# A two-FFN encoder layer on one core: plain weights ahead of the input sums, split first loads, a written order for the last tile

## The chip, the core and the metric

The kernel runs on one NeuronCore of a Trainium2 chip. The core has five engines that run side by side, each with its own queue of instructions in a fixed order: TensorE (PE) multiplies matrices into PSUM banks, with a separate weight load (PEld) ahead of each product; VectorE (DVE), ScalarE (ACT) and GpSimd (POOL) work elementwise; SyncE (SP) only issues transfers. ScalarE and GpSimd issue transfers as well. Engines wait for each other by semaphores. The metric is the device time of one execution in microseconds; lower is better.

## The reference, cut to what matters

One macaron encoder layer on two sequences of 256 rows that share all weights, so that the kernel works on 512 rows at once: an FFN with half weight, a mixer, a second FFN with half weight, and a final norm. Everything is float32.

```python
def swiglu(h, w_in, w_out):
    a, g = jnp.split(h @ w_in, [D_FF], axis=-1)       # D_FF = 2816
    return (jax.nn.silu(a) * g) @ w_out
...
    x = x + 0.5 * swiglu(rmsnorm(x, g_ffn1), w_ffn1_in, w_ffn1_out)   # x is 512 x 1024
    h = rmsnorm(x, g_mix)
    ...                                                # two scans and a gated merge
    x = x + merged.astype(x.dtype) @ w_out
    x = x + 0.5 * swiglu(rmsnorm(x, g_ffn2), w_ffn2_in, w_ffn2_out)
...
    return rmsnorm(x, g_final)
```

## The kernel before

Activations lie transposed, features on the partitions: eight tiles x0 to x7 of 128 x 512, columns 0 to 255 for one sequence and 256 to 511 for the other. A float32 product is made of three TensorE passes: weights and activations are split into a rounded half (`...h`) and a correction (`...l`), and `mm3` adds h·h, h·l and l·h. The split of a weight tile is either a ScalarE cast and a VectorE subtraction (`split2`), or (`split_dma`) a ScalarE cast, a ScalarE negated cast into the correction tile and a transfer from GpSimd's queue that adds the weights from DRAM to it; only after that transfer has landed may TensorE read the correction.

An FFN (`ffn`, called for the stages f1 and f2) has 22 pairs of output tiles (gate and value). Four parts of it matter here:

- `first_tiles`: the first three pairs (six tiles) over k = 0 to 7, as x arrives; the row scales r come from a sum of squares (`rms_stat`: GpSimd adds the squares, TensorE sums over partitions, VectorE and ScalarE take 1/sqrt, TensorE spreads the result). In f1 this part is at the program's start, where x and the first weights (`raw1`) are loaded, and where ten products on a tile of ones (`warm`) go ahead.
- two *plain* pairs (j = 3 and 4): four products of 24 matmuls each (`plain`), with weights from `w_plain`. Their tiles are p0, p1 (first pair) and p20, p21 (second).
- the other pairs (`pair`, s5 to s21 in the tile names): seven products of half width on sums of blocks of x and of weights, a fast scheme that needs `x_sums` (xc tiles) and `w_sums`. Each product is 12 matmuls. A pair issues five products and leaves the last two (`finish`) to the next pair, so the first pair has five of its own.
- the output tiles (`out_tile`), after each third of the pairs.

Weight tiles come from four rings of two buffers: `raw` and `sum` for what is loaded, `wa` and `wb` for what is split. A new tile of a ring waits until TensorE has read the last product of the tile two before it. A pair of seven products takes one buffer of each. Before, a plain pair's first tile is in wa and its second in wb:

```python
        raws = (stage["raw"].tile([P, 3, T], F32, tag="raw", name=f"raw_{name}"),
                stage["sum"].tile([P, 3, T], F32, tag="sum", name=f"sum_{name}"))
...
                      for p in w_pair("wb" if n else "wa", 2 if n else 5, f"{name}{n}"))
```

The order of the instructions on each engine is set by a scheduler when the program is built; `tc.high_priority`, `tc.issue_after(ins)` (queue behind `ins` on its engine) and `tc.manual_schedule` (keep the written order) direct it.

The last output tile of f2 (`last2`) is cut into the two column halves. Each half has 21 matmuls (`ps_f2l`), a sum of squares (`st_f`), small VectorE steps to 1/sqrt, a diagonal (`dg_f`) and its spread (`sp_f`), and four output tiles y that VectorE scales and that SP and ScalarE send out in turn.

Of the kernel before, what the change touches and what calls it, by code (L numbers as in the profile page):

```python
# [9 lines left out]
F32 = mybir.dt.float32  # L10
# [5 lines left out]
P = 128  # L16
# [20 lines left out]
def encoder_kernel(ctx: ExitStack, tc: tile.TileContext, xT, par, w2, gnorm, mask,  # L37
# [117 lines left out]
    def rms_cols(parts, cs, name, bank=None):  # L155

        ps = scp(f"st_{name}", (P, len(cs))) if bank is None else bank[:, :len(cs)]
        for i, c in enumerate(cs):
            for n, p in enumerate(parts):
                nc.tensor.matmul(ps[:, i:i + 1], lhsT=p[:, c * P:(c + 1) * P], rhs=ones[:, 0:1],  # L160
                                 start=n == 0, stop=n == len(parts) - 1)
        r = small(f"rc_{name}", len(cs))
        rsqrt(r, ps, 1.0 / D, name)
        return r

    def spread(r, name, bank=None):

# [4 lines left out]
        ps = scp(f"sp_{name}", (P, n * P)) if bank is None else bank  # L172
        nc.tensor.matmul(ps, lhsT=ones, rhs=dg.rearrange("p c t -> p (c t)"), start=True, stop=True)
        return ps

# [46 lines left out]
    def split2(hi, lo, src):  # L222
        nc.scalar.copy(hi, src)
        nc.vector.tensor_tensor(out=lo, in0=src, in1=hi.bitcast(F32), op=ALU.subtract)
# [7 lines left out]
    def first_tiles(raws, xs_of, dma_from, name):  # L232
# [3 lines left out]
        for kp in range(4):  # L236
# [3 lines left out]
            for i in range(2):  # L240
# [4 lines left out]
                if kp < dma_from:  # L245
# [14 lines left out]
        return pss, xs  # L260

    def x_sums(gcol, r, name):
# [4 lines left out]
        for k in range(4):  # L267
# [15 lines left out]
            for n, src in enumerate((v, t, w)):  # L283
                hl = [slab(f"xc{p}_{name}{k}{n}", F32R) for p in "hl"]
                split2(*hl, src)
# [6 lines left out]
    def w_sums(w_a, j, name):  # L292
# [8 lines left out]
        nc.gpsimd.dma_start(al[:, 0:2].rearrange("p a b -> p (a b)"), w_a[2 * j], accum_op=ALU.add)  # L301
        nc.vector.tensor_tensor(out=sm[:, 1], in0=sm[:, 0], in1=raw[:, 2], op=ALU.add)
# [25 lines left out]
    def w_plain(w_a, j, name):  # L328

        raws = (stage["raw"].tile([P, 3, T], F32, tag="raw", name=f"raw_{name}"),  # L330
                stage["sum"].tile([P, 3, T], F32, tag="sum", name=f"sum_{name}"))
        res = []
        for n, raw in enumerate(raws):
            raw = raw[:, 0:2].rearrange("p a b -> p (a b)")
            nc.sync.dma_start(raw, w_a[2 * j + n])
            hi, lo = (p.rearrange("p a b -> p (a b)")[:, :2 * T]
                      for p in w_pair("wb" if n else "wa", 2 if n else 5, f"{name}{n}"))
# [13 lines left out]
    def ffn(w_a, w_o, xs_of, raws, dma_from, gcol, sq, name, done, last=None):  # L351
# [3 lines left out]
        late = []  # L355
# [13 lines left out]
        def pair(j, w):  # L369
# [4 lines left out]
            nc.scalar.copy(m[:, L], y[:, :SEQ])  # L374
# [71 lines left out]
        for _ in range(3):  # L446
            next(steps)
# [601 lines left out]
```

## Time and profile before

| | |
|---|---|
| median of 3 runs | 1207.92 us (1207.36 to 1208.99) |
| the profiled execution, its own time | 1207.96 us |
| its span in the trace, first to last instruction | 1206.2 us |
| TensorE busy | 1177.4 us, 98% of the span |
| VectorE, ScalarE, GpSimd busy | 61%, 50%, 10% |
| read from HBM | 135.51 MB, 114 GB/s over the span |

Times in the rows are microseconds from the span's start. The profiled execution is 1.8 us longer than its span, the same amount in a comparison of the two kernels, so sums over the span can be set against its own time. A product's busy time is modelled to its end, past the start of the next; how fast products go is read from their starts. PEclk is the granted clock of TensorE as a share of 2.4 GHz; it has two levels, 1.00 and 0.50 (1.2 GHz).

### The profile page before, as it was taken

The page shows a single profiled execution, that of the slowest core. Times are in us where ns is not written, and L with a number is a line of the kernel's source. Part 1 is how long each engine was busy: PE and PEld are TensorE (multiplying, and loading weights), DVE is VectorE, ACT ScalarE, POOL GpSimd, SP SyncE. Part 2 cuts the span into 40 slices and gives each one's busy share as a digit, 9 for nine tenths or more (in the row PEclk, how much of TensorE's full clock was granted, in tenths as well). Part 3 has the DMA queues.
Part 4 walks back from the last instruction along what each step waited for, and adds up shares of the span by engine and source line. Part 5 has one row for each costly group of instructions (what it writes and reads, how often), then busy time and mean ns, then how long its engine had stood idle before and what let it go on. Part 6 is the DMA issues. An engine that isn't in the chain of part 4 may idle for free.

```text
span 1206.2 us, 16870 instructions
## 1 busy us (share of the span) xinstructions
PE 1177.4 (98%) x6651; PEld 1019.8 (85%) x6651; DVE 736.0 (61%) x1127; ACT 609.0 (50%) x989; POOL 114.9 (10%) x130
## 2 busy tenths in 40 slices
PE   8999999999999998999999999999989999999996
PEld 6798899899987887888888888888879899989985
DVE  6974576567547888657573453463585467566643
ACT  6753365256536655575762332244555256336541
POOL 4100000000021004020000000013100000000011
PEclk9999999999999999999999999999989999999997
DMA  7853555356414214232253223232754356446512
GB/s 236 192 137 112 130 141 139 116 132 164 125 53 127 88 37 131 71 105 70 79 184 114 91 93 114 81 94 44 184 141 130 101 134 156 132 119 154 139 46 70
DMA packets 57952, 141.88 MB, mean 118 GB/s; under 512 B 5320, under 2 KB 19656, under 8 KB 57872
## 3 DMA queue, kind: packets, MB, share of 16 engines
q1 hardware_dynamic: 47904, 110.38, 29.4%
q0 software_dynamic: 8160, 28.06, 13.4%
q10 hardware_dynamic: 1808, 2.36, 0.6%
q8 instruction: 52, 0.85, 0.3%
q14 instruction: 28, 0.23, 0.1%
HBM read 135.51 MB, written 2.11 MB: 114 GB/s over the span
## 4 chain that ended last, share of the span: by engine, by line
PE 89%; DVE 5%; DMA 2%; issue 2%; ACT 1%; SPq 1%; POOL 0%; POOLq 0%; DVEq 0%
PE psy_f L318 16%; PE psq_f L318 8%; PE psz_f L318 4%; PE ps_f1o L203 3%; PE ps_f1o L204 3%; PE ps_f1o L202 3%; PE ps_f2o L203 3%; PE ps_f2o L202 3%; PE ps_f2o L204 3%; PE ps_f2i L258 3%; PE pt_ga L545 2%; PE pt_ga L543 2%; PE pt_ga L544 2%; PE pt_gb L545 2%; PE pt_gb L543 2%; PE pt_gb L544 2%
## 5 line engine op out<-in xcount | busy, mean ns | idle before, releaser
L318 PE MATMUL psy_f<-xch_f,wal_f1s 128*128 128x256 f32 x204 | 57.3, 281 | 0.0
L318 PE MATMUL psy_f<-xcl_f,wah_f1s 128*128 128x256 f32 x204 | 57.2, 281 | 0.0
L318 PE MATMUL psy_f<-xch_f,wah_f2s 128*128 128x256 f32 x204 | 57.2, 281 | 0.0
L318 PE MATMUL psy_f<-xcl_f,wah_f2s 128*128 128x256 f32 x204 | 57.2, 281 | 0.0
L318 PE MATMUL psy_f<-xch_f,wal_f2s 128*128 128x256 f32 x204 | 57.2, 280 | 0.0
L318 PE MATMUL psy_f<-xch_f,wah_f1s 128*128 128x256 f32 x204 | 57.2, 281 | 0.0
L543 PE MATMUL pt_ga<-whi_ga,xh_m 128*128 128x512 f32 x128 | 50.7, 396 | 0.0
L545 PE MATMUL pt_ga<-whi_ga,xl_m 128*128 128x512 f32 x128 | 50.7, 396 | 0.0
L545 PE MATMUL pt_gb<-whi_gb,xl_m 128*128 128x512 f32 x128 | 50.5, 396 | 0.0
L544 PE MATMUL pt_ga<-wlo_ga,xh_m 128*128 128x512 f32 x128 | 50.4, 394 | 0.0
L543 PE MATMUL pt_gb<-whi_gb,xh_m 128*128 128x512 f32 x128 | 50.4, 394 | 0.0
L544 PE MATMUL pt_gb<-wlo_gb,xh_m 128*128 128x512 f32 x128 | 50.4, 394 | 0.0
L94 DVE TENSOR_TENSOR wlo_ga<-raw_ga,whi_ga 128x1024 fp32r<-128x1024 f32 x16 | 19.6, 1224 | 46.0 <-ACT whi_ga L93 46.0
L404 DVE SCALAR_TENSOR_TENSOR x<-ps_f2o,x 128x512 f32<-128x512 f32 x23 | 15.8, 689 | 41.6 <-PE ps_f2o L204 41.6
L93 ACT CAST whi_gb<-raw_gb 128x1024 fp32r<-128x1024 f32 x16 | 16.8, 1048 | 45.7 <-PE pt_ga L545 29.5
L94 DVE TENSOR_TENSOR wlo_gb<-raw_gb,whi_gb 128x1024 fp32r<-128x1024 f32 x16 | 19.6, 1222 | 32.7 <-ACT whi_gb L93 32.6
L318 PEld LDWEIGHTS psy_f<-xch_f,wah_f1s 128*128 128x128 f32 x204 | 38.4, 189 | 0.1
L318 PEld LDWEIGHTS psy_f<-xcl_f,wah_f2s 128*128 128x128 f32 x204 | 38.4, 188 | 0.1
L318 PEld LDWEIGHTS psy_f<-xcl_f,wah_f1s 128*128 128x128 f32 x204 | 38.4, 188 | 0.1
L318 PEld LDWEIGHTS psy_f<-xch_f,wal_f1s 128*128 128x128 f32 x204 | 38.5, 189 | 0.0
L318 PEld LDWEIGHTS psy_f<-xch_f,wah_f2s 128*128 128x128 f32 x204 | 38.3, 188 | 0.1
L318 PEld LDWEIGHTS psy_f<-xch_f,wal_f2s 128*128 128x128 f32 x204 | 38.4, 188 | 0.0
(1155 smaller groups left out, 4039.1 us busy)
## 6 DMA issues: line engine op xcount, KB each, us to landing
raw_f1s<-in_w_f SPq DMA_DIRECT2D x17, 512.0 KB, 3.7
wal_f1s<-in_w_f POOLq DMA_DIRECT2D x17, 512.0 KB, 5.5
raw_f2s<-in_w_f SPq DMA_DIRECT2D x17, 512.0 KB, 3.7
wal_f2s<-in_w_f POOLq DMA_DIRECT2D x17, 512.0 KB, 5.7
raw_ga<-in_w_tm SPq DMA_DIRECT2D x16, 512.0 KB, 3.6
raw_gb<-in_w_tm SPq DMA_DIRECT2D x16, 512.0 KB, 3.6
sum_f1s<-in_w_f SPq DMA_DIRECT2D x17, 256.0 KB, 3.3
raw_f1s<-in_w_f SPq DMA_DIRECT2D x17, 256.0 KB, 4.0
```

Of the source, the lines that this page charges most:

```text
L93: nc.scalar.copy(hi[:, :width], raw[:, :width])
L94: nc.vector.tensor_tensor(out=lo[:, :width], in0=raw[:, :width], in1=hi.bitcast(F32)[:, :width], op=ALU.subtract)
L202: nc.tensor.matmul(ps, lhsT=wh, rhs=xh, start=start, stop=False)
L203: nc.tensor.matmul(ps, lhsT=wh, rhs=xl, start=False, stop=False)
L204: nc.tensor.matmul(ps, lhsT=wl, rhs=xh, start=False, stop=stop)
L258: nc.tensor.matmul(pss[m], lhsT=w[:, f[m]], rhs=xp, start=k == n == 0, stop=k == KD - 1 and n == 2)
L318: nc.tensor.matmul(ps, lhsT=l[:, f], rhs=m, start=start and k == n == 0, stop=stop and k == 3 and n == 2, skip_group_check=True)
L404: nc.vector.scalar_tensor_tensor(out=x[i], in0=ps, scalar=0.5, in1=x[i], op0=ALU.mult, op1=ALU.add)
L543: nc.tensor.matmul(pss[t], lhsT=xh, rhs=hi[:, ws], start=k == 0, stop=False)
L544: nc.tensor.matmul(pss[t], lhsT=xh, rhs=lo[:, ws], start=False, stop=False)
L545: nc.tensor.matmul(pss[t], lhsT=xl, rhs=hi[:, ws], start=False, stop=k == KD - 1)
```

## The change

Four things are changed, three of them in both FFNs.

`w_plain` makes a plain pair's first tile in wb and its second in wa, and `ffn` writes the first plain pair's weights ahead of the input sums and the second's ahead of their last part. The weights of the first seven-product pair (s5) are queued on VectorE behind the last input sum (`issue_after(sums_done)`). Of the second (s6), the loads and the first split (`w_rows`) stay where they were, and the sums are queued on ScalarE behind the first pair's copy m. For k = 0 the weights' split is cut into two halves of three tiles.

At the start x0 comes on SP, the first half of the first weights and the parameters `pt` on ScalarE's queue, an activation on one column loads ScalarE's table early, there are 14 warming products, and the first rounded tile xh_a0 is made on VectorE.

In the last tile the order is written out: both halves' matmuls, the first half's statistics among the second half's matmuls, then the second half's statistics, and only then the outputs of both.

```diff
-    nc.scalar.dma_start(x[0], xT[0:P, :])
-    nc.gpsimd.dma_start(pt, par)
     for k in range(KD):
-        if k:
-            nc.sync.dma_start(x[k], xT[k * P:(k + 1) * P, :])
-        nc.sync.dma_start(raw1[k // 2][:, k % 2], w_f1[0:NF, :, k * P:(k + 1) * P].rearrange("m p f -> p m f"))
+        nc.sync.dma_start(x[k], xT[k * P:(k + 1) * P, :])
+        for n in ((range(0, 3), range(3, NF)) if k == 0 else (range(NF),)):
+            (nc.scalar if k == n[0] == 0 else nc.sync).dma_start(
+                raw1[k // 2][:, k % 2, n[0]:n[-1] + 1],
+                w_f1[n[0]:n[-1] + 1, :, k * P:(k + 1) * P].rearrange("m p f -> p m f"))
+        if k == 0:
+            nc.scalar.dma_start(pt, par)
+
+    act0 = cp.tile([P, 1], F32, name="act0")
+    nc.scalar.activation(act0, ones[:, 0:1], AF.Copy, scale=2.0)
 
     warm = scp("warm", (P, P))
-    for _ in range(10):
+    for _ in range(14):
...
-        nc.scalar.activation(hi, x[k], AF.Copy, scale=col(gcol + k))
+        if name == "a" and k == 0:
+            nc.vector.tensor_scalar(out=hi, in0=x[k], scalar1=col(gcol + k), scalar2=None, op0=ALU.mult)
+        else:
+            nc.scalar.activation(hi, x[k], AF.Copy, scale=col(gcol + k))
...
-                if kp < dma_from:
+                if k == 0:
+                    for h in (slice(0, 3 * P), slice(3 * P, NF * P)):
+                        split2(whi[:, h], wlo[:, h], raw[:, i, h])
+                elif kp < dma_from:
                     split2(whi, wlo, raw[:, i])
...
-        raws = (stage["raw"].tile([P, 3, T], F32, tag="raw", name=f"raw_{name}"),
-                stage["sum"].tile([P, 3, T], F32, tag="sum", name=f"sum_{name}"))
         res = []
-        for n, raw in enumerate(raws):
-            raw = raw[:, 0:2].rearrange("p a b -> p (a b)")
+        for n, (get, pool, w) in enumerate(((w_sum, "wb", 2), (w_raw, "wa", 5))):
+            raw = get(f"{name}{n}")[:, 0:2].rearrange("p a b -> p (a b)")
             nc.sync.dma_start(raw, w_a[2 * j + n])
...
         steps = x_sums(gcol, r, name)
-        for _ in range(3):
+        w_p = w_plain(w_a, NP, f"{name}p")
+        for _ in range(4):
             next(steps)
-        w_p = w_plain(w_a, NP, f"{name}p")
-        next(steps)
         gated(top, pss[2 * top], pss[2 * top + 1])
+        w_p2 = w_plain(w_a, NP + 1, f"{name}p2")
         xc += next(steps)
+        sums_done = x_last[0]
         plain(banks[0], w_p)
-        w_p = w_plain(w_a, NP + 1, f"{name}p2")
         gated(0, pss[0], pss[1])
-        nxt = units[0][0]()
+        with tc.issue_after(sums_done):
+            nxt = units[0][0]()
...
-            cur, nxt = nxt, units[n + 1][0]() if n + 1 < len(units) else None
-            run(cur)
+            cur = nxt
+            if n == 0:
+                j = NP + 3
+                rows = w_rows(w_a, j, f"{name}s{j}")
+                run(cur)
+                with tc.issue_after(copied[0]):
+                    nxt = w_sums(w_a, j, f"{name}s{j}", rows)
+            else:
+                nxt = units[n + 1][0]() if n + 1 < len(units) else None
+                run(cur)
...
+        with tc.manual_schedule(engines={nc.tensor.engine, nc.vector.engine, nc.scalar.engine}):
+            mms(0, range(n))
+            final(0)
+            mms(1, range(n // 2 + 1))
+            st = [rms_sum([sq_of("f"), sql], (0, 1), "f0")]
+            mms(1, range(n // 2 + 1, n))
+            rc = [small(f"rc_f{half}", 2) for half in range(2)]
+            rsqrt(rc[0], st[0], 1.0 / D, "f0")
+            final(1)
+            dg = [diag(rc[0], "f0")]
+            st.append(rms_sum([sq_of("f"), sql], (2, 3), "f1"))
+            rf = [broadcast(dg[0], "f0")]
+            rsqrt(rc[1], st[1], 1.0 / D, "f1")
+            dg.append(diag(rc[1], "f1"))
+            rf.append(broadcast(dg[1], "f1"))
+            for half in range(2):
+                scaled(half, rf[half])
```

`rms_sum`, `diag`, `broadcast` and `w_rows` are parts of `rms_cols`, `spread` and `w_sums`, cut out so that they can be called apart. `mms`, `final` and `scaled` are the three parts of the old loop over the halves.

How the order on the engines moves, at three places. First TensorE in the second FFN, where the second plain product ends and the third begins (ps_f2p1 is the second's bank, ps_f2p2 the third's). Before:

```order
L202 MATMUL ps_f2p1_7648<-xh_b7_7454,wbh_f2p1_7729 128x512
L203 MATMUL ps_f2p1_7648<-xl_b7_7455,wbh_f2p1_7729 128x512
L204 MATMUL ps_f2p1_7648<-xh_b7_7454,wbl_f2p1_7730 128x512
L202 MATMUL ps_f2p2_7875<-xh_b0_7171,wah_f2p20_7840 128x512
L203 MATMUL ps_f2p2_7875<-xl_b0_7172,wah_f2p20_7840 128x512
L204 MATMUL ps_f2p2_7875<-xh_b0_7171,wal_f2p20_7841 128x512
```

and with the change:

```order
L220 MATMUL ps_f2p1_7659<-xh_b7_7463,wah_f2p1_7690 128x512
L221 MATMUL ps_f2p1_7659<-xl_b7_7464,wah_f2p1_7690 128x512
L222 MATMUL ps_f2p1_7659<-xh_b7_7463,wal_f2p1_7691 128x512
L220 MATMUL ps_f2p2_7886<-xh_b0_7180,wbh_f2p20_7778 128x512
L221 MATMUL ps_f2p2_7886<-xl_b0_7181,wbh_f2p20_7778 128x512
L222 MATMUL ps_f2p2_7886<-xh_b0_7180,wbl_f2p20_7779 128x512
```

The order of the four products was wa, wb, wa, wb and is wb, wa, wb, wa, so the second pair's wa tile is read last.

Second, ScalarE in the second FFN around the first and second seven-product pairs (f2s5, f2s6: their weights; f20hh to f24hh: activations of the first five pairs; f2m5, f2u5: copies of the first seven-product pair out of PSUM). Before:

```order
L431 ACTIVATE f2t3_7945<-f2t3_7945 128x512
L299 CAST wah_f2s6_7970<-raw_f2s6_7965 128x1024
L223 CAST f20hh_7931<-f2t0_7851 128x512
L431 ACTIVATE f2t4_7955<-f2t4_7955 128x512
L300 ACTIVATE wal_f2s6_7971<-raw_f2s6_7965 128x1024
L223 CAST f21hh_7936<-f2t1_7925 128x512
L223 CAST wah_f2s6_7970<-sum_f2s6_7966 128x1536
L223 CAST f22hh_7941<-f2t2_7760 128x512
L223 CAST wbh_f2s6_7972<-raw_f2s6_7965 128x1024
L223 CAST f23hh_7951<-f2t3_7945 128x512
L374 COPY f2m5_7986<-psy_f25_7984 128x256
L223 CAST f24hh_7961<-f2t4_7955 128x512
```

and with the change:

```order
L456 ACTIVATE f2t4_7966<-f2t4_7966 128x512
L241 CAST f22hh_7952<-f2t2_7771 128x512
L241 CAST f23hh_7962<-f2t3_7956 128x512
L322 CAST wah_f2s6_7981<-raw_f2s6_7976 128x1024
L323 ACTIVATE wal_f2s6_7982<-raw_f2s6_7976 128x1024
L399 COPY f2m5_7990<-psy_f25_7988 128x256
L241 CAST wah_f2s6_7981<-sum_f2s6_7977 128x1536
L241 CAST f24hh_7972<-f2t4_7966 128x512
L402 ACTIVATE f2t5_7992<-f2t5_7992 128x256
L241 CAST wbh_f2s6_7983<-raw_f2s6_7976 128x1024
L406 COPY f2u5_7991<-psy_f25_7988 128x256
```

The four casts of the second pair's weights moved from before the activations to behind them, with the first pair's copies m and u between and behind them.

Third, VectorE in the last tile (x7: the last tile of x, one half at a time; the number behind f is the half). Before:

```order
L944 SCALAR_TENSOR_TENSOR x7_85<-ps_f2l1_10833,x7_85 128x256
L149 TENSOR_SCALAR v_f0_10807<-st_f0_10801 128x2
L150 RECIPROCAL rc_f0_10806<-s_f0_10808 128x2
L946 TENSOR_TENSOR sql_10776<-x7_85 128x256
L151 TENSOR_TENSOR s_f0_10808<-rc_f0_10806 128x2
L152 SCALAR_TENSOR_TENSOR s_f0_10808<-s_f0_10808,v_f0_10807 128x2
L153 SCALAR_TENSOR_TENSOR rc_f0_10806<-s_f0_10808,rc_f0_10806 128x2
L171 TENSOR_SCALAR dg_f0_10815<-pt_77,rc_f0_10806 128x128 x2
L952 TENSOR_TENSOR y00_10820<-xg00_10562,sp_f0_10818 128x512
```

and with the change:

```order
L158 SCALAR_TENSOR_TENSOR rc_f0_10841<-s_f0_10844,rc_f0_10841 128x2
L982 SCALAR_TENSOR_TENSOR x7_85<-ps_f2l1_10789,x7_85 128x256
L984 TENSOR_TENSOR sql_10787<-x7_85 128x256
L179 TENSOR_SCALAR dg_f0_10853<-pt_77,rc_f0_10841 128x128 x2
L154 TENSOR_SCALAR v_f1_10863<-st_f1_10856 128x2
L155 RECIPROCAL rc_f1_10842<-s_f1_10864 128x2
L156 TENSOR_TENSOR s_f1_10864<-rc_f1_10842 128x2
L157 SCALAR_TENSOR_TENSOR s_f1_10864<-s_f1_10864,v_f1_10863 128x2
L158 SCALAR_TENSOR_TENSOR rc_f1_10842<-s_f1_10864,rc_f1_10842 128x2
L179 TENSOR_SCALAR dg_f1_10871<-pt_77,rc_f1_10842 128x128 x2
L992 TENSOR_TENSOR y00_10876<-xg00_10573,sp_f0_10861 128x512
```

The first half's small steps no longer wait for the second half's x7, and the second half's small steps stand ahead of the first output y00 where they stood behind the fourth.

## Rows read from the trace of the kernel before

**Rows 1.** The page's busy time by engine over the whole span.
```profile
PE 1177.4 (98%) x6651; PEld 1019.8 (85%) x6651; DVE 736.0 (61%) x1127; ACT 609.0 (50%) x989; POOL 114.9 (10%) x130
```

**Rows 2.** TensorE's waits over the span: total us, times, longest us.
```profile
PE ps_f2p L204 <- DMA wal_f2p<-in_w_f: 4.9, 1, 4.9
...
PE sp_f L173 <- DVE dg_f L171: 4.6, 2, 2.6
```

**Rows 3.** Timeline of the second FFN: start us, us, engine, line, operation, [idle before].
```profile
856.64 0.85 POOL L230 DMA_DIRECT2D wbl_f2p<-in_w_f  x1 [3.43 <-ACT xch_f L223]
...
869.99 0.69 DVE L302 TENSOR_TENSOR sum_f2s<-sum_f2s,raw_f2s 128x512 f32<-128x512 f32 x1 [10.90 <-DMA raw_f2s<-in_w_f]
...
875.50 1.05 ACT L229 ACTIVATE wal_f2p<-raw_f2p 128x1024 fp32r<-128x1024 f32 x1
...
876.85 0.85 POOL L230 DMA_DIRECT2D wal_f2p<-in_w_f  x1 [16.31 <-ACT wal_f2p L229]
...
884.51 0.80 PE L204 MATMUL ps_f2p<-xh_b,wal_f2p 128*128 128x512 f32 x1 [4.93 <-DMA wal_f2p<-in_w_f]
...
889.77 0.39 PE L204 MATMUL ps_f2p<-xh_b,wal_f2p 128*128 128x512 f32 x1
```

**Rows 4.** One stretch of the windows view: busy by engine, PEclk, DMA share, GB/s.
```profile
886.00:888.00 2.00, 2.00 (x6) 1.61 (x5) 2.00 (x5) 0.00 (x0) 0.00 (x0) 0.50 0.97 254
```

**Rows 5.** Timeline of the first FFN: the wait among the plain products.
```profile
60.54 0.50 PE L204 MATMUL ps_f1p<-xh_a,wal_f1p 128*128 128x512 f32 x1 [1.76 <-DMA wal_f1p<-in_w_f]
```

**Rows 6.** Timeline of the first FFN's first two pairs of seven products.
```profile
72.73 0.28 PE L318 MATMUL psz_f<-xch_f,wah_f1s 128*128 128x256 f32 x1
...
78.60 1.05 ACT L299 CAST wah_f1s<-raw_f1s 128x1024 fp32r<-128x1024 f32 x1 [0.99 <-PE psy_f L318]
...
79.81 0.28 PE L318 MATMUL psz_f<-xch_f,wah_f1s 128*128 128x256 f32 x1
...
81.17 0.85 POOL L301 DMA_DIRECT2D wal_f1s<-in_w_f  x1 [11.78 <-ACT wal_f1s L300]
```

**Rows 7.** Tile view of wal_f1s: its transfers from issue to landing.
```profile
DMA to landing us min/median/max: 5.3/5.5/7.5
```

**Rows 8.** Timeline of the program's start.
```profile
1.00 4.63 PE L129 MATMUL warm<-ones 128*128 128x128 f32 x20 [1.00 <-POOL ones L99]
...
8.14 2.19 PE L258 MATMUL ps_f1i<-xh_a,wbh_f1i 128*128 128x512 f32 x6 [2.51 <-ACT wbh_f1i L223]
...
14.00 1.55 PE L258 MATMUL ps_f1i<-xh_a,wbh_f1i 128*128 128x512 f32 x6
...
18.19 1.57 PE L258 MATMUL ps_f1i<-xh_a,wah_f1i 128*128 128x512 f32 x6
...
18.24 4.95 POOL L199 TENSOR_TENSOR sq<-sq,sq_a 128x512 f32<-128x512 f32 x3 [0.43 <-ACT sq_a L198]
...
19.75 0.62 ACT L198 ACTIVATE sq_a<-x 128x512 f32<-128x512 f32 x1
...
27.94 1.10 PE L173 MATMUL ps_f1p<-dg_f,ones 128*128 128x512 f32 x2 [1.46 <-DVE dg_f L171]
```

**Rows 9.** Windows view of a stretch in the start.
```profile
10.00:12.00 2.00, 2.00 (x6) 1.51 (x6) 1.76 (x3) 2.00 (x4) 1.42 (x1) 0.50 1.13 321
```

**Rows 10.** Timeline of the last tile.
```profile
1187.52 0.38 PE L160 MATMUL st_f<-ones,sqf 128*128 128x1 f32 x2 [0.39 <-POOL sqf L199]
...
1194.24 1.88 DVE L952 TENSOR_TENSOR y<-xg,sp_f 128x512 f32<-128x512 f32 x3 [1.11 <-PE sp_f L173]
...
1195.56 6.93 SPq L957 DMA_DIRECT2D out_yT<-y  x4
```

**Rows 11.** Windows view of three half-microseconds in the output's transfer.
```profile
1196.50:1197.00 0.50, 0.00 (x0) 0.00 (x0) 0.49 (x3) 0.00 (x0) 0.00 (x0) 0.50 1.00 338
...
1199.50:1200.00 0.50, 0.00 (x0) 0.00 (x0) 0.50 (x1) 0.00 (x0) 0.00 (x0) 0.50 0.14 43
...
1201.00:1201.50 0.50, 0.00 (x0) 0.00 (x0) 0.50 (x2) 0.00 (x0) 0.00 (x0) 0.50 0.77 252
```

More of the change, by code (lines that the diff above doesn't have):

```diff
@@ L161, in rms_cols, with diag @@
                                  start=n == 0, stop=n == len(parts) - 1)
+        return ps
+    def rms_cols(parts, cs, name, bank=None):
         r = small(f"rc_{name}", len(cs))
-        rsqrt(r, ps, 1.0 / D, name)
+        rsqrt(r, rms_sum(parts, cs, name, bank), 1.0 / D, name)
         return r
-    def spread(r, name, bank=None):
+    def diag(r, name):
         n = r.shape[-1]
@@ L171, in spread, with broadcast @@
             nc.vector.tensor_scalar(out=dg[:, c, :], in0=ident, scalar1=r[:, c:c + 1], scalar2=None, op0=ALU.mult)
-        ps = scp(f"sp_{name}", (P, n * P)) if bank is None else bank
+        return dg
+    def broadcast(dg, name, bank=None):
+        ps = scp(f"sp_{name}", (P, dg.shape[1] * P)) if bank is None else bank
         nc.tensor.matmul(ps, lhsT=ones, rhs=dg.rearrange("p c t -> p (c t)"), start=True, stop=True)
         return ps
+    def spread(r, name, bank=None):
+        return broadcast(diag(r, name), name, bank)
     def rms_stat(sq, name, banks=(None, None)):
@@ L301, in w_sums @@
         nc.gpsimd.dma_start(al[:, 0:2].rearrange("p a b -> p (a b)"), w_a[2 * j], accum_op=ALU.add)
+        return raw, sm, ah, al, bh, bl
+    def w_sums(w_a, j, name, rows=None):
+        raw, sm, ah, al, bh, bl = rows or w_rows(w_a, j, name)
         nc.vector.tensor_tensor(out=sm[:, 1], in0=sm[:, 0], in1=raw[:, 2], op=ALU.add)
@@ L354, in ffn @@
         add = lambda o, p, q: nc.vector.tensor_tensor(out=o, in0=p, in1=q, op=ALU.add)
-        late = []
+        late, copied = [], []
         hs = []
@@ L373, in pair @@
             product(y, w[0], xc[X11], True, False)
-            nc.scalar.copy(m[:, L], y[:, :SEQ])
+            copied.append(nc.scalar.copy(m[:, L], y[:, :SEQ]).ins)
             product(z, w[1], xc[X21], True, True)
@@ L937, in last2, with mms, final, scaled @@
         n = len(hs)
-        for half in range(2):
-            cs = slice(half * SEQ, (half + 1) * SEQ)
-            ps = acc(f"ps_f2l{half}")[:, :SEQ]
-            for k in range(n):
+        cut = [slice(0, SEQ), slice(SEQ, T)]
+        pss = [acc(f"ps_f2l{half}")[:, :SEQ] for half in range(2)]
+        def mms(half, ks):
+            for k in ks:
                 f = slice(k * P, (k + 1) * P)
-                mm3(ps, hi[:, f], lo[:, f], hs[k][0][:, cs], hs[k][1][:, cs], k == 0, k == n - 1)
-            nc.vector.scalar_tensor_tensor(out=x[i][:, cs], in0=ps, scalar=0.5, in1=x[i][:, cs],
+                mm3(pss[half], hi[:, f], lo[:, f], hs[k][0][:, cut[half]], hs[k][1][:, cut[half]], k == 0, k == n - 1)
+        def final(half):
+            cs = cut[half]
+            nc.vector.scalar_tensor_tensor(out=x[i][:, cs], in0=pss[half], scalar=0.5, in1=x[i][:, cs],
                                            op0=ALU.mult, op1=ALU.add)
             nc.vector.tensor_tensor(out=sql[:, cs], in0=x[i][:, cs], in1=x[i][:, cs], op=ALU.mult)
-            rf = spread(rms_cols([sq_of("f"), sql], (2 * half, 2 * half + 1), f"f{half}"), f"f{half}").unsqueeze(1)
+        def scaled(half, rf):
+            cs, rf = cut[half], rf.unsqueeze(1)
             for n_ in range(KD // 2):
```

14 lines of the change are left out of this document (7 added, 7 removed).

## The prediction

> **What bounds the kernel now.** I read the page first, then TensorE's waits, then the timelines round each wait. The page shows TensorE busy for 1177.4 of 1206.2 us [rows 1]: whatever the change does to the other engines counts only where TensorE waits, runs at the lower clock, or has finished and the output still drains. The list of waits has one large entry, 4.9 us in the second FFN, and two near the end, 4.6 us together [rows 2]. Four places are left, and the change touches all four.
>
> *Second FFN, plain products.* TensorE stands still for 4.93 us until the correction half wal_f2p of the second plain pair has landed, and starts again at 884.51 [rows 3]. ScalarE wrote that tile only at 875.50 and the accumulating transfer went out at 876.85, because VectorE had stood for 10.90 us, until 869.99, at the first addition of the seven-product weights, and the gate products on which ScalarE's queue hangs were behind it [rows 3]. After the wait the granted clock is 0.50, 1.2 instead of 2.4 GHz [rows 4]; the full pace is back at 889.77 [rows 3].
>
> *First FFN, same place.* The same wait, 1.76 us [rows 5].
>
> *Start.* The warming products end at 5.63, the first real product starts at 8.14 after 2.51 us of idling, and its first 18 products take until 14.00; the next 18 take until 18.19 [rows 8]. Between them the clock is at 0.50, while the transfers run at 321 GB/s with all engines busy [rows 9]. Later TensorE waits 1.46 us for the spread of the row scales [rows 8].
>
> *End.* The two column halves of the last tile go one after the other; the output of the first flows at 338 GB/s, nearly stops, and the second's follows [rows 11].
>
> **The change part by part.** All sums are against the profiled execution, 1207.96 us; the median of the runs shown is 1207.92, so it stands for them.
>
> (1) Plain pair first, wb before wa. The tile that was late was in the third of four plain products and is now in the fourth. A product is 24 matmuls; at full clock 18 take 18.19 - 14.00 = 4.19 us [rows 8], so 24 take 5.6. Even if it landed no earlier than at 884.51, it would be needed at 884.51 - 4.93 + 5.6 = 885.2. It will land earlier as well, since ScalarE now writes it before two casts of the input sums, and VectorE no longer blocks at 869.99. What is now third, the wb tile of that pair, had its transfer issued at 856.64 [rows 3], 23 us before 879.6. So the wait goes: 4.93 us. With it goes the slow clock: 884.51 to 889.77 is 5.26 us for 12 matmuls that take 2.79 at full pace, so 2.47 us. Together 7.4. In the first FFN 1.76 goes by the same shift (the need moves from 58.8 to 64.4, the landing was at 60.5 [rows 5]); the clock did not fall there. Bounds: nothing, if the tile is still late, and 7.4 and 1.8, since a wait cannot give more than itself.
>
> (2) The other side of (1). The wa buffers are two, and the second pair of seven products (s6) needs the one that the second plain pair holds. That was free one product before the plain part's end; now its product is the last, and ScalarE's cast for s6 waits for the very end. Behind it on ScalarE stand the copy m, the cast of the sums, the activation of the first pair and the copies u, for which TensorE's fourth and fifth products of that pair wait. The price by the nearest rows: the third pair's weights have the same wait already. The second pair begins 12 matmuls before 79.81, at 78.40; the cast starts at 78.60 and the transfer is issued at 81.17 [rows 6], 2.77 us after the buffer came free. It lands 5.3 to 7.5 us later, median 5.5 [rows 7]: 8.27 us after the plain part ends. The first pair has only five products, 79.81 - 72.73 = 7.08 us [rows 6], and the third matmul of the next reads the tile, 0.24 later. So a new wait of 8.27 - 7.32 = 0.95 us in each FFN; I take 0.95, twice 1.9. Bounds from the landings: 0.75 and 2.95 each; one copy less stands ahead in ScalarE's queue, which could take a little off. If the copy u is the late one, the wait is moved forward and not added, because the tile's transfer goes on meanwhile.
>
> The Trainium skill (DMA: Bandwidth & Descriptors, "Anatomy of one DMA") puts a transfer from GpSimd's queue at about 2.0 us plus its bytes at 436 GB/s; for these 512 KB that is an estimate of 3.2 us, by which the tile would be there 2.77 + 3.2 = 6.0 us after the end, no wait would open and the sum below would be 1195.2. The accumulating transfers of this trace took 5.3 at the least [rows 7], so the measurement decides, and the page's case is a rival below.
>
> (3) Start. Four more warming products, x0 first on SP, half of the first weights and the parameters on ScalarE's queue, the activation table loaded ahead, xh_a0 on VectorE. TensorE can then start at about 1.00 + 14 x 0.463 = 7.5 without the idling [rows 8], and the clock may not fall: at most 0.66 + 1.67 = 2.3 us. But the next thing in TensorE's order is the sum of squares. It is ready when GpSimd's last addition ends, 18.24 + 4.95 = 23.19, three additions of 1.65 [rows 8]. The last square was written at 19.75 + 0.62 = 20.37 and the input comes in at a full 321 GB/s [rows 8, 9], so it can hardly be earlier; but GpSimd was behind by 21.54 - 20.37 = 1.17, and a ScalarE that is freed of the table and of xh_a0 should let it catch up. The chain from there to the spread at 27.94 is unchanged, so I take 1.17, rounded 1.2. Bounds: 0, and 2.3. The half casts for k = 0 add two ScalarE and two VectorE instructions in each FFN; in the first they are in the start's term, in the second TensorE shows no wait near them, so nothing; without that cover, under 1 us.
>
> (4) Last tile. The wait of 0.39 us for sqf [rows 10] lies behind the second half's products now, and both halves' statistics stand ahead of the first output. Before, the second half's data began to flow at about 1201.5 - 0.5 x 252/340 = 1201.1, when the first half's had ended at about 1199.6 [rows 11]: 1.5 us of silence, which goes, since the second half's outputs follow without a pause. The first output was ready at 1194.24 + 0.69, but the first transfer went out at 1195.56 [rows 10], because ScalarE's queue held the square root of the second half first; that is now done before, so 0.6 more. The first output itself I put 0.3 earlier, by estimate: the second half's small steps now stand ahead of it, but everything before them starts earlier by the 0.39 and by the gaps that the statistics made among the products. Sum 2.4. Bounds: -0.2, if it starts later by as much as TensorE once waited for such steps, 2.6 [rows 2], and 2.5, if it gains the whole 0.39.
>
> Everything else (the order constraint, the renamed helpers, a few reordered transposes) moves no wait of [rows 2]: nothing.
>
> Sum: 1207.96 - 7.4 - 1.8 + 1.9 - 1.2 - 2.4 = 1197.1.
>
> **The rivals.**
> *The start gives nothing, or costs.* TensorE arrives earlier at a sum of squares that the loads set, and idles there some 1.3 us and again before the spread; after 4.93 us the clock fell, after 1.76 it did not. Without the 1.2 it is 1198.3; with a fall as dear as 2.47 on top of the gain, 1199.6. The full transfer rate speaks for it. The Trainium skill (Trainium Kernel Development and Optimization, Key Constraints) says that transfers from all issuing queues run on the same 16 engines, so that spreading them saves issue time alone; it is the same warning.
> *The new wait is long*: landings of 7.5 us, 2.95 in each FFN, 1201.1. For it: such a landing is in [rows 7].
> *No new wait*: the tile lands within 4.55 us, or the queue ahead is shorter. 1195.2. Against: the least is 5.3.
> *The wait in the second FFN stays*: 7.4 lost, 1204.5. Against: the shift by a whole product.
> *The output does not close up*: 2.4 lost, 1199.5.
> *Slower.* At the first pairs a wait opens that is as dear as the old one in the second FFN, 7.4 with its slow clock, in both: without (2) the gains are 12.8, so 12.8 - 14.8 gives 1210.0. It decides from 6.4 us each; that needs a tile 13.7 us after the plain part's end.
>
> **How the numbers follow.** Forecast as summed, 0.50 (own range 1195.5 to 1198.8); start 0.15; long wait 0.10; no wait 0.12; wait stays 0.05; output 0.04; slower 0.04. The prediction is the first, 1197.1. From 1194.0 to 1201.5 lie all but the last two mishaps and the edges of the others, about 0.8. A measurement of this kernel tells about 0.2%, 2.4 us: faster is below 1205.5, which all but the slower rival and half of the stayed wait give: 0.93; same 0.05; slower 0.02.
>
> **What would show it.** (1) No wait of a product on wal_f2p or wal_f1p, and clock 1.00 through the second FFN's plain part. (2) A wait at the second pair's first product on wal_f1s and wal_f2s, or on a copy u, near 1 us. (3) No slow clock before 14 us, a wait at the sum of squares, and the spread 1.2 earlier. (4) Output transfers in one stretch of about 6 us. It would be wrong if a wait on wal_f2p remains, if the wait under (2) is over 3 us or brings the clock down, or if the spread of the start is not earlier than 27.

## The result and the profile after

The changed kernel takes 1195.66 us (median of 4 runs, 1194.58 to 1196.52) against 1208.38 us before (4 runs): ratio 0.9894, 95% interval 0.9879 to 0.9909. Predicted were 1197.1 us, range 1194.0 to 1201.5. The profiled execution took 1196.41 us with a span of 1194.6, so 11.6 us less of span than before.

TensorE's waits after the change (total us, times, longest us), to be read beside [rows 2]:

```profile
PE pt_vg L578 <- DVE wlo_vg L94: 3.8, 2, 2.6
PE ps_f1p L165 <- POOL sq L217: 2.0, 1, 2.0
PE sp_f L184 <- DVE dg_f L179: 1.3, 1, 1.3
...
PE st_f L165 <- DVE sql L984: 0.9, 1, 0.9
...
PE psy_f L346 <- ACT f1u L406: 0.4, 1, 0.4
PE psy_f L346 <- DMA wal_f2s<-in_w_f: 0.3, 1, 0.3
```

No product waits for wal_f2p or wal_f1p any more. New are the line on sq, 2.0 us at the sum of squares in the start, and the two last, at the second seven-product pairs. In the last tile the waits for the spreads (sp_f) fell from 4.6 to 1.3 us, and 0.9 us on the second half's squares (sql) is new.

The timeline of the second FFN shows why the first is gone; [rows 3] are the rows before:

```profile
866.46 1.05 ACT L247 ACTIVATE wal_f2p<-raw_f2p 128x1024 fp32r<-128x1024 f32 x1
867.80 0.87 POOL L248 DMA_DIRECT2D wal_f2p<-in_w_f  x1 [8.65 <-ACT wal_f2p L247]
883.60 0.40 PE L222 MATMUL ps_f2p<-xh_b,wal_f2p 128*128 128x512 f32 x1
888.72 0.28 PE L346 MATMUL psy_f<-xch_f,wah_f2s 128*128 128x256 f32 x1
```

ScalarE writes the late tile at 866.46 instead of 875.50, its transfer goes out at 867.80 instead of 876.85, and the product that reads it comes at 883.60. Over the plain part the granted clock is 1.00 (columns as in [rows 4]):

```profile
866.00:889.00 23.00, 23.00 (x102) 18.68 (x101) 20.74 (x32) 13.58 (x20) 1.73 (x2) 1.00 0.57 149
```

The start in the timeline, beside [rows 8], and two stretches of it in the windows view, beside [rows 9]. The sum of squares before:

```profile
23.25 1.05 PE L160 MATMUL ps_f1p<-ones,sq 128*128 128x1 f32 x8
```

and with the change, with GpSimd's last additions and ScalarE's last square ahead of it:

```profile
12.29 9.37 POOL L217 TENSOR_TENSOR sq<-sq,sq_a 128x512 f32<-128x512 f32 x5 [0.53 <-ACT sq_a L216]
18.51 0.62 ACT L216 ACTIVATE sq_a<-x 128x512 f32<-128x512 f32 x1
21.71 1.71 PE L165 MATMUL ps_f1p<-ones,sq 128*128 128x1 f32 x8 [1.98 <-POOL sq L217]
24.71 2.76 PE L279 MATMUL ps_f1i<-xh_a,wal_f1i 128*128 128x512 f32 x6
27.27 1.76 PE L184 MATMUL ps_f1p<-dg_f,ones 128*128 128x512 f32 x2
46.99 0.39 PE L220 MATMUL ps_f1p<-xh_a,wbh_f1p 128*128 128x512 f32 x1
```

```profile
10.00:12.00 2.00, 2.00 (x10) 1.62 (x9) 2.00 (x2) 2.00 (x4) 1.34 (x1) 1.00 1.12 369
22.00:24.00 2.00, 2.00 (x9) 1.90 (x10) 2.00 (x4) 0.50 (x1) 0.00 (x0) 0.50 0.00 0
1190.00:1191.00 1.00, 0.00 (x0) 0.00 (x0) 0.88 (x3) 0.00 (x0) 0.00 (x0) 0.50 1.09 382
```

The sum of squares comes 1.54 us earlier than before, but TensorE, which got there 3.5 us earlier, idled 1.98 us for it, and then the granted clock is 0.50: six matmuls take 2.76 us instead of 1.55 [rows 8]. The spread, at 27.27, is only 0.67 us earlier than before, and by the plain part, at 46.99, nothing is left of the lead (47.01 before). The third line is the output at the end: 382 GB/s where [rows 11] have about 340. Its first transfer is issued 10.2 us after the last tile's first product (1176.27), against 11.1 us before (1195.56 [rows 10], first product at 1184.48):

```profile
1186.47 4.09 ACTq L997 DMA_DIRECT2D out_yT<-y  x4
```

Between fixed places of TensorE's order the two profiled spans differ so (us, worked out from the first matmul of each place):

| stretch | before | after | difference | predicted |
|---|---|---|---|---|
| start, to the first plain product of the first FFN | 47.01 | 46.99 | -0.0 | -1.2 |
| its four plain products | 24.31 | 22.28 | -2.0 | -1.8 |
| from there to the second product of the second seven-product pair | 8.49 | 9.23 | +0.7 | +0.95 |
| plain products of the second FFN | 29.84 | 22.30 | -7.5 | -7.4 |
| to the second product of its second seven-product pair | 8.48 | 9.23 | +0.75 | +0.95 |
| last tile's first product to the end of the span | 21.72 | 18.33 | -3.4 | -2.4 |

All other stretches together differ by 0.1.

### The profile page after: what moved, and what is told of

Its sections match the earlier page's. It is cut to its first block, busy times and chain, and to the rows that moved or that the text cites. A ratio compares the mean times of both kernels' runs of the same rounds, so it can differ in the third digit from the quotient of the medians.

```text
span 1194.6 us, 16893 instructions
## 1 busy us (share of the span) xinstructions
PE 1176.0 (98%) x6659; PEld 1019.4 (85%) x6659; DVE 736.5 (62%) x1130; ACT 609.2 (51%) x991; POOL 117.8 (10%) x129
## 4 chain that ended last, share of the span: by engine, by line
PE 90%; DVE 5%; DMA 2%; ACT 1%; issue 1%; POOL 1%; SPq 0%; DVEq 0%; POOLq 0%; ACTq 0%
PE psy_f L346 16%; PE psq_f L346 8%; PE psz_f L346 4%; PE ps_f1o L221 3%; PE ps_f1o L222 3%; PE ps_f1o L220 3%; PE ps_f2o L221 3%; PE ps_f2o L220 3%; PE ps_f2o L222 3%; PE ps_f2i L279 3%; PE pt_ga L579 2%; PE pt_ga L577 2%; PE pt_ga L578 2%; PE pt_gb L579 2%; PE pt_gb L577 2%; PE pt_gb L578 2%
## 5 line engine op out<-in xcount | busy, mean ns | idle before, releaser
L94 DVE TENSOR_TENSOR wlo_ga<-raw_ga,whi_ga 128x1024 fp32r<-128x1024 f32 x16 | 19.6, 1224 | 46.4 <-ACT whi_ga L93 46.4
L94 DVE TENSOR_TENSOR wlo_gb<-raw_gb,whi_gb 128x1024 fp32r<-128x1024 f32 x16 | 19.6, 1224 | 32.7 <-ACT whi_gb L93 32.6
L429 DVE SCALAR_TENSOR_TENSOR x<-ps_f1o,x 128x512 f32<-128x512 f32 x24 | 16.6, 690 | 36.2 <-PE ps_f1o L222 36.2
```

The lines of the kernel that those rows point to most:

```text
L94: nc.vector.tensor_tensor(out=lo[:, :width], in0=raw[:, :width], in1=hi.bitcast(F32)[:, :width], op=ALU.subtract)
L429: nc.vector.scalar_tensor_tensor(out=x[i], in0=ps, scalar=0.5, in1=x[i], op0=ALU.mult, op1=ALU.add)
```

## The experiments

Each is an edit of the changed kernel unless it says otherwise. Four ran on one chip (order_only, early_only, start_old, tail_old), four on a second (swap_f2, start_later, tail2, pt_pool), three on a third (best, after_again, w0_whole), before_x0 on a fourth. Times are medians, of 4 executions but for before_x0, with the ratio to the kernel before on the same chip and its interval.

**The plain products.** *order_only* keeps the order wb, wa and the old places of preparation:

```diff
-        w_p = w_plain(w_a, NP, f"{name}p")
-        for _ in range(4):
+        for _ in range(3):
             next(steps)
+        w_p = w_plain(w_a, NP, f"{name}p")
+        next(steps)
...
-        w_p2 = w_plain(w_a, NP + 1, f"{name}p2")
...
         plain(banks[0], w_p)
+        w_p2 = w_plain(w_a, NP + 1, f"{name}p2")
```

> The changed kernel with wb ahead of wa in both plain pairs, but with the two pairs prepared where the kernel before prepares them (the first after three of the four input sums, the second after the first pair's products). Theory A, of the prediction: the later place of the wa product alone is enough, since the late tile landed 16.7 us after the plain part's start and is now needed 17.4 us after it: no wait on wal_f2p, time within 0.5 us of the changed kernel (1196.4 in its profile). Rival: the early preparation is what does it; then wal_f2p is waited for again, by 1 to 5 us with the clock falling at the long end, time 1197.5 to 1203.9.

Measured 1195.92 (0.9893, interval 0.9877 to 0.9909), and no wait on wal_f2p, as theory A has it. But the run doesn't test A, because the tile came earlier too. Its transfer went out between the 876.85 of before and the 867.80 of the changed kernel:

```profile
870.41 0.87 POOL L248 DMA_DIRECT2D wal_f2p<-in_w_f  x1 [10.94 <-ACT wal_f2p L247]
871.36 0.68 DVE L330 TENSOR_TENSOR sum_f2s<-sum_f2s,raw_f2s 128x512 f32<-128x512 f32 x1
```

With the longest landing of this tile, 7.5 us, it was there at 877.9; the third place, counted from this run's plain part (866.73), would have read it at about 878.3. In the first FFN the old order would have waited 0.2 us at most (issued at 51.12, landed 8.1 us later at the latest, third place at about 59.0). What came with the old places of preparation is the order constraint on the first seven-product weights: VectorE adds them at 871.36, behind the input sums and without waiting, where in [rows 3] it stood 10.90 us for them. What the constraint does alone was not tried.

*early_only* keeps the early preparation and turns the order back to wa, wb (`((w_raw, "wa", 5), (w_sum, "wb", 2))` in w_plain).

> The changed kernel with the early preparation, but wa ahead of wb in both plain pairs as before. In the changed kernel the second pair's wal_f2p landed at about 875 and would be needed in third place at about 878; in the first FFN it landed at about 58.4 and would be needed at 58.6. Theory A (each half of the edit is enough by itself): no wait on either, or one under 0.5 us in the first FFN; and as the wa buffer is free one product earlier, the new wait at the second seven-product pair (0.75 us in each FFN) goes: 1194.9. Rival: the order is needed: the old waits are back, 1.8 and 4.9 us and the slow clock, 1203 to 1206.

Measured 1195.90 (0.9892, 0.9877 to 0.9907). In the profiled execution no product waits on wal_f1p or wal_f2p, and the new wait is gone: from the first product of the first seven-product pair to the second product of the second it takes 8.50 us in both FFNs. These two rows are the ends of it in the second FFN:

```profile
888.52 0.28 PE L346 MATMUL psy_f<-xch_f,wah_f2s 128*128 128x256 f32 x1
897.02 0.28 PE L346 MATMUL psz_f<-xch_f,wah_f2s 128*128 128x256 f32 x1
```

So the order is not needed when the tiles are made early, and without it the new wait is gone. The mechanism is as expected, the 1.5 us don't show in the median. Two of the four executions took 1196.4 although their mean clock was the higher one; where they lost it was not profiled.

*swap_f2* turns the order round for one pair only: `w_plain(w_a, NP + 1, ..., (wa, wb) if name == "f2" else (wb, wa))`.

> The changed kernel with one product order turned round: in the second FFN alone the second plain pair multiplies wa ahead of wb. The wa buffer that the second seven-product pair needs is then free one product (5.6 us) before the plain part ends. Theory A (the new wait comes from that buffer alone): from the first product of the first seven-product pair to the second product of the second takes 8.50 us in the second FFN, as before the change, instead of 9.23; no wait on wal_f2p, which landed at 875 and is needed at 878; time 0.75 us below the changed kernel's like executions. Rival: the wait is the queue of casts on ScalarE or the transfer's own length, and it stays: 9.2 us again, no gain.

Measured 1193.74 (0.9884, 0.9869 to 0.9899). The second FFN has 8.50 us again (887.75 to 896.25). The cast that waited for the buffer is early now; its rows in this kernel and, in the second fence, in the changed one:

```profile
882.15 1.05 ACT L322 CAST wah_f2s<-raw_f2s 128x1024 fp32r<-128x1024 f32 x1 [1.23 <-PE ps_f2p L221]
```

```profile
888.68 1.05 ACT L322 CAST wah_f2s<-raw_f2s 128x1024 fp32r<-128x1024 f32 x1 [1.99 <-PE ps_f2p L221]
```

It ran 5.6 us before the plain part's end at 887.75 in the one, and at its very end (888.72) in the other. So the new wait comes from the wa buffer. In the time of the whole 0.75 us is too little to tell from the spread.

**The start.** *start_old* has the start of the kernel before.

> The changed kernel with the start of the kernel before (its loads, ten warming products, no activation table ahead, x0 scaled on ScalarE, whole casts for k = 0). Theory: the start gives nothing, since the plain part began at 46.99 in the changed kernel and at 47.01 before; what the earlier sum of squares gains, TensorE's clock loses after the wait for it: time the same within 0.5 us, and the low clock again near 9 to 12 us instead of near 22 to 28. Rival, the prediction's own term: the start is worth 1.2 us and the time is 1.2 us longer, 1197.6.

Measured 1196.54 (0.9897, 0.988 to 0.9914): the same, by the median. The low clock was back at the first products: the view of the granted clock shows 1.00 there, but six matmuls take 2.7 us from one start to the next, and the pace is full only from 13.28 on:

```profile
8.00 2.93 PE L268 MATMUL ps_f1i<-xh_a,wbh_f1i 128*128 128x512 f32 x6 [2.36 <-ACT wbh_f1i L233]
10.72 2.76 PE L268 MATMUL ps_f1i<-xh_a,wbl_f1i 128*128 128x512 f32 x6
13.28 1.67 PE L268 MATMUL ps_f1i<-xl_a,wbh_f1i 128*128 128x512 f32 x6
```

At the sum of squares and at the spread it stayed at full pace, the plain part began at 46.44, 0.55 earlier than in the changed kernel, and more than that was lost in the output, which flowed at the old rate though the tail was the new one:

```profile
10.00:12.00 2.00, 2.00 (x6) 1.52 (x5) 1.76 (x3) 2.00 (x4) 1.56 (x1) 1.00 1.14 322
1188.00:1190.00 2.00, 0.00 (x0) 0.00 (x0) 1.93 (x5) 0.00 (x0) 0.00 (x0) 0.50 1.03 338
```

From the last tile's first product to the end it took 19.6 us, against 18.3 in the changed kernel. The time came out as expected, but with a lead and a loss that the expectation didn't have.

*start_later* holds two things back on TensorE:

```diff
+            with tc.issue_after(mark["f1i", 3, 1]):   # after the wl products of column tile 3
                 rc = rms_cols([sq], range(4), name, banks[0])
+            with tc.issue_after(mark["f1i", 4, 1]):   # after those of tile 4
                 ps = spread(rc, name, banks[1])
```

> The changed kernel with the sum of squares of the first FFN held back on TensorE until the wl products of the fourth column tile are through, and the spread until the wl products of the fifth. Theory A (the start's gain was lost to the low clock after TensorE's idle time at the sum of squares): TensorE idles under 1 us ahead of the sum and under 0.5 us ahead of the spread, the clock stays at 1.00 from 6 us on, the plain part begins at 45.0 to 45.4 instead of 46.99, and the runs stay together near 1194.6 instead of lying in two heaps 1.8 us apart. Rival: the idle time is not what brings the clock down; then it falls again somewhere before 31 us, the plain part begins near 47, and the runs spread as before.

Measured 1192.38 (0.9873, 0.9858 to 0.9888; 1192.14 to 1193.34). The timeline has no idle time at the sum nor at the spread, and the clock stays:

```profile
20.28 1.54 PE L284 MATMUL ps_f1i<-xh_a,wal_f1i 128*128 128x512 f32 x6
21.65 0.95 PE L165 MATMUL ps_f1p<-ones,sq 128*128 128x1 f32 x8
22.46 1.65 PE L284 MATMUL ps_f1i<-xl_a,wah_f1i 128*128 128x512 f32 x6
...
26.82 1.10 PE L184 MATMUL ps_f1p<-dg_f,ones 128*128 128x512 f32 x2
...
41.73 0.39 PE L223 MATMUL ps_f1p<-xh_a,wbh_f1p 128*128 128x512 f32 x1
```

```profile
24.00:31.00 7.00, 7.00 (x30) 5.13 (x29) 1.75 (x10) 6.21 (x9) 2.59 (x4) 1.00 0.93 226
```

Theory A, and more than it: the plain part begins at 41.73, 5.3 us earlier. The theory had counted the clock alone, 1.6 to 2.0 us. tail_old, below, has the start of the changed kernel and kept the full pace there; it idled 1.7 us at the sum and 1.5 at the spread and began the plain part at 45.04. So 3.3 of the 5.3 us are idle time, which matmuls with their inputs ready now fill, and 2.0 are the clock. Not all of it reaches the end: in the first FFN the new wait at the second seven-product pair grows (from the first product of the first pair to the second product of the second it takes 10.06 us instead of 9.23), and the last tile takes 0.6 us longer. The profiled execution is 4.1 us shorter.

**The last tile and the transfer rate.** *tail_old* has last2 of the kernel before.

> The changed kernel with the last tile as before. From the traces the end is worth 3.4 us: first output 0.9 earlier, the pause in the output 1.6, and 0.9 that the prediction didn't have; in that the output flows at 384 instead of 340 GB/s. Theory A: the faster rate belongs to the output going in one stretch, and the old tail flows at about 340 on this chip too: 1199.8. Theory B: the rate is that of the chip or of the execution, not of the edit: then it is the same with the old tail as with the new one on this chip, and the old tail costs about 2.5 to 2.7: 1199.0.

Measured 1197.24 (0.9904, 0.9889 to 0.9919). From the last tile's first product to the end it took 20.8 us, 2.5 more than in the changed kernel, and the old tail, with its pause, flowed at the new rate:

```profile
1186.00:1187.00 1.00, 0.00 (x0) 0.00 (x0) 0.79 (x6) 0.00 (x0) 0.00 (x0) 0.50 1.09 385
1188.00:1190.00 2.00, 0.59 (x2) 0.00 (x0) 1.37 (x3) 0.00 (x0) 0.00 (x0) 0.50 0.00 0
1191.00:1192.00 1.00, 0.00 (x0) 0.00 (x0) 0.24 (x1) 0.00 (x0) 0.00 (x0) 0.50 1.09 384
```

Theory B, with one correction that start_old gives: the rate is not the chip's (both ran on the same one) but comes with the start's edits. The time is lower than either theory's, which were counted from the changed kernel's profiled execution with its low clock; the profiled execution here, 1196.50, kept the full pace in the same start and began the plain part at 45.04.

*pt_pool*, *w0_whole* and *before_x0* look for the edit that sets the rate. The first loads the parameters from `nc.gpsimd`, the second the first weights whole on `nc.sync`; the third is the kernel before with x0 on `nc.sync`:

```diff
-    nc.scalar.dma_start(x[0], xT[0:P, :])
...
-        if k:
-            nc.sync.dma_start(x[k], xT[k * P:(k + 1) * P, :])
+        nc.sync.dma_start(x[k], xT[k * P:(k + 1) * P, :])
```

> The changed kernel with one thing of its start undone: the parameter table is loaded from GpSimd's queue instead of ScalarE's. With the old start all transfers at full load ran at 308 to 335 GB/s in the start and 340 in the output; with the new one at 345 to 383 and 384, whatever the tail. Theory A (the parameter table's queue sets the rate): about 320 and 340 again, the sum of squares near 23.2 instead of 21.7, time 0.7 to 2 us longer. Theory B (x0 on the first queue, or the split of the first weights, does it): the rates stay at about 365 and 384, time the same.

> The changed kernel with the first weights in one transfer on the first queue, behind x0, instead of in halves on two queues. The parameter table's queue did not change the rate (345 to 383 GB/s in the start, 381 to 388 in the output, whichever queue). Theory A (the split of the first weights over two queues sets the rate): 308 to 335 GB/s in the start and 340 in the output, time 0.7 us longer by the output and more by the start. Theory B (where x0 goes sets it): the rates stay at 345 to 383 and 384; the first real product starts later, at about 7.5, and the time moves by less than 0.5 us.

> The kernel before with one thing changed: x0 goes first on the first queue like the other seven, instead of on ScalarE's. Neither the parameter table's queue nor the split of the first weights moved the transfer rate, so x0's place is left. Theory A (it sets the rate): 345 to 383 GB/s in the start instead of 308 to 335, 384 in the output instead of 340, the squares' last addition and so the sum of squares near 22 instead of 23.25, and by the output alone 2.1 MB / 340 - 2.1 MB / 384 = 0.7 us less, with up to 1.3 us more from the start: 1206 to 1207.3 beside the kernel before. Rival (it takes several of the start's edits, or another one of them): rates as before, time the same.

The same two kinds of stretch in each, pt_pool, w0_whole and before_x0 in this order:

```profile
10.00:12.00 2.00, 2.00 (x11) 1.61 (x10) 2.00 (x3) 2.00 (x5) 1.31 (x2) 1.00 1.12 369
1189.00:1190.00 1.00, 0.00 (x0) 0.00 (x0) 0.60 (x2) 0.00 (x0) 0.00 (x0) 0.50 1.09 386
```

```profile
10.00:12.00 2.00, 2.00 (x10) 1.59 (x9) 1.88 (x2) 2.00 (x4) 1.77 (x2) 1.00 1.12 368
1187.00:1188.00 1.00, 0.00 (x0) 0.00 (x0) 1.00 (x3) 0.00 (x0) 0.00 (x0) 0.50 1.09 385
```

```profile
10.00:12.00 2.00, 2.00 (x6) 1.52 (x6) 1.86 (x3) 2.00 (x4) 1.16 (x1) 1.00 1.14 323
1202.00:1203.00 1.00, 0.36 (x1) 0.36 (x2) 0.48 (x2) 0.00 (x0) 0.00 (x0) 0.50 1.04 348
```

pt_pool 1195.56 (0.9901, 0.9885 to 0.9918) and w0_whole 1194.16 (0.9884, 0.987 to 0.9899) keep the high rate; w0_whole began the first product at 5.75, not at the expected 7.5, and the changed kernel, with the split loads, at 6.21, so the split earns nothing. before_x0 keeps the low rate and is 0.2% slower than the kernel before, 1210.71 (12 executions; 1.0021, 1.0012 to 1.0031). So the high rate stays when the parameters' queue or the split alone is undone, and x0's queue alone does not bring it. Which of the start's edits, alone or together, do bring it stays open.

*tail2* reorders the last tile once more: the first half's diagonal ahead of the second half's additions, its spread ahead of the second half's sums, two of its outputs ahead of the second root.

> The changed kernel with another order in the last tile: the first half's diagonal ahead of the second half's additions, its spread ahead of the second half's sums, and its first two outputs ahead of the second half's reciprocal root. In the changed kernel the first output is issued at 10.2 us after the last tile's first product, and the output then takes 8.1 us, of which 5.5 are transfer at 384 GB/s. Theory A (the end is set by when the outputs become ready on VectorE): first issue near 8.4 us after the first product, last one 0.5 earlier, end 0.5 to 1.4 us earlier. Rival (only the transfer counts, and a pause opens between the halves): the same within 0.3 us.

Measured 1194.54 (0.989, 0.9875 to 0.9905). The first output was issued 8.2 us after the last tile's first product; a pause opened between the halves:

```profile
1186.00:1187.00 1.00, 0.14 (x1) 0.14 (x2) 0.86 (x5) 0.00 (x0) 0.00 (x0) 1.00 1.06 373
1187.00:1188.00 1.00, 0.80 (x2) 0.16 (x2) 1.00 (x3) 0.00 (x0) 0.00 (x0) 0.59 0.02 4
```

From the last tile's first product to the end it took 17.9 us, 0.4 less: theory and rival each hold in part.

**All that gained, together**, beside the changed kernel on the same chip.

> The three edits that gained, together: wa ahead of wb in the second plain pair of the second FFN, the sum of squares and the spread of the first FFN held back on TensorE, and the other order in the last tile. Theory (they act at three places that don't touch): from the held-back sum alone, 1192.4, less 0.75 at the second FFN's second seven-product pair and less 0.4 in the last tile: 1191.2, with the clock at 1.00 until the last tile in all runs, which then lie within 1.5 us. Rival: TensorE, which comes earlier, finds a wait of another kind in the second FFN or at the end, and the time stays above 1192.

> The changed kernel itself once more, on the chip of the best one, to compare like with like. Theory of the low clock: its runs lie in two heaps, near 1194.6 without a low clock in the start and near 1196.4 with one, whichever comes how often. Rival: one heap, and the earlier spread was chance between chips.

*best*: 1191.27 (0.986, 0.9846 to 0.9875), four executions within 1191.12 to 1191.56, as expected and 4.1 us below the changed kernel on that chip. The rival holds at one place: in the first FFN, where the order was not turned round, the second seven-product pair's second product now comes 10.53 us after the first pair begins, 2.0 more than in the kernel before. Turning the order round there too was not tried. *after_again*: 1195.36 (0.9896, 0.9879 to 0.9912), 1194.35 to 1195.92; its profiled execution, the fastest, began the plain part at 45.37. With those first measured there are eight executions of the changed kernel: four from 1194.35 to 1194.91, with a mean granted clock of 0.994 to 0.995, and four from 1195.87 to 1196.52, with 0.993 to 0.994. That looks like the two heaps, though eight are few. It does not fit a heap without a low clock, since the fastest had one too, if a shorter one. The first line shows it in after_again; the second is the clock of best, over all its start:

```profile
24.00:26.00 2.00, 1.92 (x5) 0.99 (x3) 1.74 (x10) 2.00 (x4) 0.00 (x0) 0.50 0.75 240
6.00:40.00 34.00, 33.95 (x148) 27.00 (x149) 27.41 (x43) 26.90 (x40) 16.59 (x12) 1.00 0.96 264
```

## Why the prediction was right, and where it was not

**(1) Plain pair first.** Right in size and place: 7.5 and 2.0 against 7.4 and 1.8; the excess, 0.14 and 0.27, lies at the stops themselves, beside the idle time that the view gives. Which part of the change does it is less clear than the step has it. early_only shows that the order isn't needed. order_only doesn't show that the order alone is enough, since its tile was early as well. Both kept the order constraint, which the prediction had put at nothing without a run to show it, and which frees VectorE from its wait of 10.90 us. Whether it would have been enough by itself stays open.

**(2) The new wait.** Right, at the lower edge: 0.74 and 0.75 against 0.95, with bounds of 0.75 and 2.95 (0.6 and 0.5 in after_again). It stood partly in front of the product that waits for copy u (0.4 in the first FFN), as the step said it might. early_only and swap_f2 show that it hangs on the wa buffer. In the changed kernel the transfers of [rows 7] again took 5.3 us at the least, so the 3.2 us estimated from the Trainium skill (DMA: Bandwidth & Descriptors, "Anatomy of one DMA") doesn't hold for them.

**(3) Start.** The term that was mis-sized: -1.2 predicted, -0.0 measured in the profiled execution, -1.6 in after_again and -2.0 in tail_old, which have the same start. order_only, early_only, swap_f2 and tail2 have it too and began the plain part between 46.66 and 47.44, so -0.4 to +0.4. By the prediction's own sign, a spread not earlier than 27, the step was wrong: the spread came at 27.27. Two steps of its working failed. It held the loads, at a full 321 GB/s, to set the last square; but ScalarE is busy for 2.00 of 2.00 us in [rows 9] and has no wait from 6.65 on until that square, so that its own queue set it. The square ended 1.24 us earlier (19.13 instead of 20.37), and GpSimd, from which the whole 1.17 was to come, gave the other 0.3. That the sum came 1.54 earlier, near the 1.2, is luck.

And the step counted the idling at the first product as gone, with the clock that falls there; but TensorE, 1.9 us earlier there and 3.5 at the sum, idles 1.98 us at the sum instead, and the clock falls there.

The rival "the start gives nothing" named just that idling, at some 1.3 us, with the clock's fall on top; its time of 1198.3 was missed by 1.0 through (4) and by some 0.7 through (1) and (2). The Trainium skill (Trainium Kernel Development and Optimization, Key Constraints), cited for that rival, leaves only issue time to be saved by other queues. The trace agrees for w0_whole, where the split gave nothing; whether the 369 against 321 GB/s of the start as a whole goes against it is open, because the edit behind that rate was not found.

**(4) Last tile.** -2.4 predicted, -3.4 measured, outside its bounds. The mechanism was right: the first output goes out 0.9 us earlier, and the pause in the output is gone. The edit itself is worth 2.1 at the old rate (before 21.7, start_old 19.6) and 2.5 at the new one (tail_old 20.8, changed 18.3), so its size was right too. The remaining 0.9 to 1.25 comes with the start's edits and their faster output and was in no term; by the rates alone, 2.1 MB at 340 and at 384 GB/s, it would be 0.7. (3) promised 1.2 too much and (4) 1.0 too little, which nearly cancels, so that the sum came within 0.7 us of the profiled execution partly by luck.

## What to carry to other kernels

A buffer ring decides which product may come last: see who needs the buffer next before turning an order round. When a stage is made to start earlier, look at what the engine waits for next; where an engine keeps the order of its queue, work with its inputs ready should stand ahead of a reduction that is late, which here was worth some 3 us. A term of one or two microseconds in the start needs several executions, since its clock differs between them.

## What was not expected of the hardware

**The low clock is not the same in each execution.** A stretch at half pace follows a wait of TensorE in the first 30 us in nine profiled executions (before, changed, order_only, early_only, start_old, swap_f2, tail2, after_again, before_x0; the longest such wait of each is 1.3 to 2.6 us), but none in tail_old (1.7 and 1.5 us), pt_pool (2.3) and w0_whole (1.5). Where, after the warming products, it waited for nothing over 0.3 us, in start_later and best, the pace was full throughout. What decides in between was not found. And the shown clock is not enough to tell: in start_old and before_x0 it is 1.00 near 10 us, where six matmuls take 2.6 to 2.7 us from one start to the next instead of 1.4.

**The rate of transfers goes with the start's edits.** 321 to 323 GB/s in the start (from 10 to 12 us) goes with about 340 in the output 1,190 us later (before, start_old, before_x0), and 367 to 369 with about 384 (all others). start_old and tail_old ran on the same chip and differ in it. Which of the edits does it, and how, was not found.
